# A hybrid block on one core: attention moved ahead by pairs of heads, the matrix memory moved beside W_out

## The chip, the cores and the metric

The kernel runs on one core of one Trainium2 chip. The time is that of one execution on the device, in microseconds; three runs gave 2598.55, 2602.10 and 2604.48 us, and their median, 2602.1 us, is the time before. The profile is one more execution, whose span is 2604.3 us. A difference of 0.2%, about 5 us, is the least that such runs tell from none.

## The reference, cut to what matters

All 2048 tokens are one sequence of width 1024, and everything is float32.

```
a = rmsnorm(x); u = a @ w_in
mq, mk, mv, mo, mi, mf, sq, sk, sv = split(u)    # 4 x 512, 2 x 4, 3 x 512 columns
mq, mk = silu(conv4(mq)), silu(conv4(mk))        # causal, 4 taps
hm = sigmoid(mo) * rmsnorm(mlstm(mq, mk, mv, mi, mf))   # 4 heads x 128, a matrix memory by chunks
hs = stick_breaking(sq, sk, sv)                  # 8 heads x 64, causal
h = x + concat(hm, hs) @ w_out
h = h + hier_moe(rmsnorm(h))                     # router, 32 experts, top 2 in one of 4 groups
h = h + sigmoid(rmsnorm(h) @ w_ple_gate) * rmsnorm(p @ w_ple_proj)
out = rmsnorm(h)
```

In the stick-breaking attention each score z gives a keep factor sigmoid(-z); a query's weight on a key is the difference of two running products of these factors, taken from the query backwards.

## The kernel before, in words

A float32 product that has to be exact is three products of TensorE in float32r: each operand is split into a rounded part and the rest (`split`, L79 a copy that rounds, on ScalarE; L80 a subtraction on VectorE), and `mm3` (L88 to L90) issues hi x hi, lo x hi, hi x lo. The normalised input, transposed and split, stays in SBUF as aTh and aTl for all projections.

`phase1`, in the order of TensorE's instructions: the transposes of x (L175) with the 32 units of `out_gate` between them (24 products of 260 columns each, the output gate and the memory's gates); `gates`, a chain of small transfers and running maxima; mq and mk, four heads each, 96 products of 512 columns a head, with a convolution on VectorE behind; mv, 32 units of 24 products of 256 columns. Then `stick_proj`: 12 weight chunks of 128 columns (q, k and v of four pairs of heads), 4 units of 24 products of 512 columns each, results to DRAM. A unit of these stands between the steps of `mlstm`, which goes through 16 chunks of 128 tokens in three steps each and writes its result to DRAM (hmh, hml). `load_w` holds two sets of split weights and loads one chunk ahead; those of `stick_proj` are issued by ScalarE (L116), others by SP.

`phase2` is the attention, 320 part-steps of 128 queries by up to 512 keys. A step of `front`: two products z (L579, L580), the sigmoid on ScalarE (L582), a mask on GpSimd for a diagonal block (L584), the running product by a scan on VectorE (L587). A step of `back` on the block before: four transposes (L600), the split (L79, L80), and two products with the differences of v (L612, L613). Blocks are 512 queries t by 512 keys s; heads come in the order (1, h), then (3, h) with the (0, h), then (2, h). Between heads stand tiles of W_out of 128 tokens whose 512 queries are done: 48 products of 512 columns (L88 to L90 into `pw`), 8 transposes (L557) and 8 products of the router (L561). The last tiles of W_out, the projection of p and the routing (`after_attention`) end at 1577 us; the experts (to 2399 us) and the last stage follow, and neither is touched.

[...]

Of the kernel before, what the change touches and what calls it, by code (L numbers as in the profile page):

```python
# [30 lines left out]
def f32(ap):  # L31
    return ap.bitcast(F32)


class Net:
    def __init__(self, ctx, tc, a, out):
# [9 lines left out]
        self.zeros = self.const.tile([P, TB], F32, name="zeros")  # L46
# [45 lines left out]
    # ---------------------------------------------------------------- projections  # L92
    def phase1(self):
        nc, tc, a = self.nc, self.tc, self.a
        self.q2 = self.mk("q2", [SH, P, S])          # rows: q_hi | q_lo of a head
        self.k2 = self.mk("k2", [SH, P, 2, S])       # [k_hi ; k_hi], [k_lo ; k_lo]
        self.dv2 = self.mk("dv2", [NT, P, SH, P])    # v[s-1] - v[s], hi | lo
        self.vend = self.const.tile([64, SH, NT], F32, name="vend")     # last v row of each token tile
# [4 lines left out]
        self.hmh = self.mk("hmh", [MH, P, S])  # L103
        self.hml = self.mk("hml", [MH, P, S])
        w_in = a["w_in"][0].rearrange("(c p) n -> p c n", p=P)
        with ExitStack() as st:
            ap_ = st.enter_context(tc.tile_pool(name="aT", reuse_waits="tile", bufs=1))
            pp = st.enter_context(tc.tile_pool(name="pp1", reuse_waits="tile", bufs=4, space=PSUM))
# [5 lines left out]
            def load_raw(wp, c0, n, width):  # L114
                raw = wp.tile([P, KC, width], F32, name="wraw", bufs=1)
                (nc.scalar if n == P else nc.sync).dma_start(raw[:, :, :n], w_in[:, :, c0:c0 + n])  # L116
                return raw
# [10 lines left out]
            def proj_dt(w, m, t):  # L128
                """[128 columns, 512 tokens]"""
# [6 lines left out]
                return ps  # L136

            def proj_td(w, n, i):
                """[128 tokens, n columns]"""
# [7 lines left out]
            G = self.G = self.const.tile([P, 2, NT, MH], F32, name="G")  # L147
            bg = self.const.tile([P, 8], F32, name="bg")
            nc.gpsimd.dma_start(bg, self.rows(a["b_gates"], 8))

            def load_x(xp, t):
                """512 tokens, normalised"""
# [8 lines left out]
            def norm_x(xp, xn):  # L161
                for xt in xn:
                    sq = xp.tile([P, D], F32, name="sq", bufs=1)
                    ss = self.small.tile([P, 1], F32, name="ss")
                    last = nc.scalar.activation(sq, xt, AF.Square, accum_out=ss)
                    r = self.rstd(ss, D, 1)
                    nc.vector.tensor_scalar(xt, xt, r, None, op0=ALU.mult)
                return last.ins

            def turn_x(ptp, xn, t):  # L170
                """a^T of 512 tokens"""
# [7 lines left out]
            # gates and output gate, values: [tokens, columns]  # L179
            with tc.tile_pool(name="w1", reuse_waits="tile", bufs=2) as wp:  # L180
                def out_gate(gp, w, h, i):
                    nv = 260 if h == 0 else 252
                    ps = proj_td(w, 260, i)
                    so = gp.tile([P, 260], F32, name="so", bufs=2)
# [7 lines left out]
                with tc.tile_pool(name="og", reuse_waits="tile", bufs=1) as gp, \  # L192
                        tc.tile_pool(name="xs", reuse_waits="tile", bufs=4) as xp, \
                        tc.tile_pool(name="pt1", reuse_waits="tile", bufs=4, space=PSUM) as ptp:
                    xn = load_x(xp, 0)
                    raw = load_raw(wp, O_MO, 260, 260)
                    last = norm_x(xp, xn)
                    gmh = gp.tile([P, MW], F32, name="gmh")
                    nc.gpsimd.dma_start(gmh, self.rows(a["g_mhead"], MW))
                    w2 = None  # L200
                    for t in range(NTB):
                        turn_x(ptp, xn, t)
                        if t == 0:
                            with tc.issue_after(last):
                                w = load_w(wp, O_MO, 260, 260, raw)
                        if t + 1 < NTB:
                            xn = load_x(xp, t + 1)
                            norm_x(xp, xn)
                        for i in range(4 * t, 4 * t + 4):
                            out_gate(gp, w, 0, i)  # L210
                            if t:
                                out_gate(gp, w2, 1, i - 4)
                        w2 = w2 or load_w(wp, O_MO + 260, 260, 260)
                    for i in range(NT - 4, NT):
                        out_gate(gp, w2, 1, i)
                mg = st.enter_context(tc.tile_pool(name="mg", reuse_waits="tile", bufs=1, side="right"))
                with tc.tile_pool(name="mgs", reuse_waits="tile", bufs=1, side="right") as ms, \
                        tc.tile_pool(name="cv", reuse_waits="tile", bufs=1, side="right") as cv:
                    w = load_w(wp, O_MQ, 256, 260)
                    gates = self.gates(mg, ms, pp)  # L220
                    next(gates)
                    for dst, off, cw, sc in ((self.mqs, O_MQ, "conv_q", 1.0), (self.mks, O_MK, "conv_k", float(P) ** -0.5)):
                        taps = cv.tile([P, 4, MH], F32, name="taps" + cw)
                        for j in range(4):
                            nc.sync.dma_start(taps[:, j], a[cw][0, j].rearrange("(h p) -> p h", p=P))
                        for h in range(2):
                            nxt = {(O_MQ, 0): O_MQ + 256, (O_MQ, 1): O_MK, (O_MK, 0): O_MK + 256, (O_MK, 1): O_MV}[off, h]
                            w2 = load_w(wp, nxt, 256, 260)
                            for m in range(2):
                                hd = 2 * h + m  # L230
                                raw = cv.tile([P, 3 + S], F32, name="cvraw")
                                nc.vector.memset(raw[:, 0:3], 0.0)
                                for t in range(NTB):
                                    ps = proj_dt(w, m, t)
                                    nc.scalar.copy(raw[:, 3 + t * TB:3 + (t + 1) * TB], ps)
                                acc = cv.tile([P, S], F32, name="cvacc")
                                nc.vector.tensor_scalar(acc, raw[:, 0:S], taps[:, 0, hd:hd + 1], None, op0=ALU.mult)
                                for j in range(1, 4):
                                    nc.vector.scalar_tensor_tensor(acc, raw[:, j:j + S], taps[:, j, hd:hd + 1], acc,
                                                                   op0=ALU.mult, op1=ALU.add)  # L240
                                next(gates, None)
                                sg = raw[:, 3:]
                                nc.scalar.activation(sg, acc, AF.Sigmoid)
                                nc.vector.scalar_tensor_tensor(acc, acc, sc, sg, op0=ALU.mult, op1=ALU.mult)
                                nc.sync.dma_start(dst[hd * P:(hd + 1) * P, :], acc)
                            w = w2
                sw = st.enter_context(tc.tile_pool(name="sw", reuse_waits="tile", bufs=2, side="right"))
                with tc.tile_pool(name="mvp", reuse_waits="tile", bufs=2) as vpool:
                    for h in range(2):
                        if h == 0:  # L250
                            w2 = load_w(wp, O_MV + 256, 256, 260)
                        else:
                            w, w2 = w2, load_w(sw, O_SQ, P, P)
# [1061 lines left out]
```

## Time and profile before

| | |
|---|---|
| median of the runs | 2602.1 us (2598.55 to 2604.48) |
| profiled execution, span | 2604.3 us, 36320 instructions |
| TensorE busy | 2440.4 us, 94% |
| VectorE busy | 1718.2 us, 66% |
| ScalarE busy | 1296.2 us, 50% |
| GpSimd busy | 658.9 us, 25% |
| read and written | 385.44 MB and 114.39 MB |

The profile counts an engine as busy while at least one of its instructions runs. A product on TensorE is recorded until its result is out, and the next starts before that, so that the spacing of products, not their recorded length, says what one costs. "Idle before" is the time an engine did nothing before an instruction, with what ended it. The span falls into stages by TensorE's work: 0 to 412 us the input, the output gate, mq, mk and mv; 412 to 770 `stick_proj` and the matrix memory; 770 to 1515 the attention with W_out; and the untouched rest.

### The profile page before, as it was taken

What the parts mean: (1) busy time and instruction counts of PE and PEld (TensorE: products, weight loads), DVE (VectorE), ACT (ScalarE), POOL (GpSimd) and SP (SyncE); (2) the same over time, 40 slices, a digit from 0 to 9 for tenths busy, and PEclk for the clock granted to TensorE, in tenths of its full rate; (3) what the DMA queues carried; (4) which work ended last, traced back from release to release, by engine and by line L of the source; (5) the groups of instructions that cost most, each with busy time, mean ns of one, the idle gap of its engine ahead of it and who ended that gap; (6) DMA issues with size and microseconds to landing.
All of it is one profiled execution on the core that took longest, in us unless ns stands there. A gap on an engine that the chain in (4) does not pass through costs nothing. (4 is left out here: it accounts for less than half of the span.)

```text
span 2604.3 us, 36320 instructions
## 1 busy us (share of the span) xinstructions
PE 2440.4 (94%) x12620; PEld 1986.2 (76%) x12620; DVE 1718.2 (66%) x2623; ACT 1296.2 (50%) x2249; POOL 658.9 (25%) x777
## 2 busy tenths in 40 slices
PE   7989999999987898889999998999999999998998
PEld 7968899888776666666777776778877778776887
DVE  4335412444549999998787566877677778776665
ACT  5322212322336666656454355666566667665443
POOL 2200000100113333322222122332332233231664
PEclk9999999999998999999999998999999999999999
DMA  5231125677766566555555548999999899998332
GB/s 181 90 47 71 66 88 144 186 207 219 211 158 158 152 157 163 139 138 144 146 146 142 146 154 274 305 309 312 299 281 327 285 307 313 310 309 268 131 132 97
DMA packets 333013, 502.25 MB, mean 193 GB/s; under 512 B 39644, under 2 KB 176988, under 8 KB 331804
## 3 DMA queue, kind: packets, MB, share of 16 engines
q1 hardware_dynamic: 210540, 338.57, 39.5%
q0 software_dynamic: 97616, 123.05, 20.6%
q10 hardware_dynamic: 24672, 38.29, 4.2%
q8 instruction: 100, 1.64, 0.3%
q14 instruction: 85, 0.70, 0.1%
HBM read 385.44 MB, written 114.39 MB: 192 GB/s over the span
## 5 line engine op out<-in xcount | busy, mean ns | idle before, releaser
L80 DVE TENSOR_TENSOR wl<-wraw,wh 128x1024 fp32r<-128x1024 f32 x384 | 457.9, 1218 | 122.1 <-ACT wh L79 118.6
L79 ACT CAST wh<-wraw 128x1024 fp32r<-128x1024 f32 x384 | 396.8, 1051 | 214.9 <-DMA wraw<-in_w_exp_up_dram 66.4
L88 PE MATMUL ppx<-wh,xh 128*128 128x512 f32 x816 | 330.2, 405 | 2.1 <-ACT wh L79 1.6
L90 PE MATMUL ppx<-wh,xl 128*128 128x512 f32 x816 | 323.4, 397 | 2.8 <-DVE xl L80 2.7
L89 PE MATMUL ppx<-wl,xh 128*128 128x512 f32 x816 | 322.5, 396 | 0.5 <-DVE wl L80 0.5
L88 PE MATMUL ps<-aTh,whi 128*128 128x512 f32 x640 | 255.2, 399 | 0.0
L89 PE MATMUL ps<-aTl,whi 128*128 128x512 f32 x640 | 254.8, 398 | 0.0
L90 PE MATMUL ps<-aTh,wlo 128*128 128x512 f32 x640 | 254.1, 397 | 0.0
L600 PE MATMUL pt<-ident,prod 128*128 128x128 f32 x1088 | 191.8, 289 | 61.5 <-DVE pl L80 55.5
L587 DVE TENSOR_TENSOR_SCAN prod<-keep,prod,zeros 128x512 f32<-128x512 f32 x192 | 244.2, 1273 | 1.7 <-ACT keep L582 0.6
L600 PEld LDWEIGHTS pt<-ident,prod 128*128 128x128 f32 x1088 | 124.8, 143 | 149.8 <-DVE pl L80 132.6
L79 ACT CAST ph<-pt 128x512 fp32r<-128x512 f32 (+1 forms) x320 | 166.7, 522 | 141.0 <-PE pt L600 137.7
L582 ACT ACTIVATE keep<-pz 128x512 f32<-128x512 f32 (+2 forms) x320 | 170.7, 536 | 58.9 <-PE pz L580 38.3
L80 DVE TENSOR_TENSOR pl<-pt,ph 128x512 fp32r<-128x512 f32 (+1 forms) x320 | 186.3, 585 | 5.7 <-ACT ph L79 5.5
L90 PEld LDWEIGHTS ppx<-wh,xl 128*128 128x128 f32 x816 | 154.5, 189 | 40.5 <-DVE xl L80 5.4
L88 PEld LDWEIGHTS ppx<-wh,xh 128*128 128x128 f32 x816 | 154.6, 189 | 36.5 <-ACT wh L79 2.0
L89 PEld LDWEIGHTS ppx<-wl,xh 128*128 128x128 f32 x816 | 154.8, 190 | 33.4 <-DVE wl L80 1.0
L1105 POOL DMA_INDIRECT h<-y,tokd x47 | 125.7, 2675 | 161.1 <-DVE y L1104 61.0
L88 PE MATMUL ps<-whi,aTh 128*128 128x260 f32 (+1 forms) x512 | 145.7, 285 | 0.0
L89 PE MATMUL ps<-wlo,aTh 128*128 128x260 f32 (+1 forms) x512 | 144.8, 283 | 0.0
L90 PE MATMUL ps<-whi,aTl 128*128 128x260 f32 (+1 forms) x512 | 143.7, 283 | 0.0
L72 POOL TENSOR_TENSOR rs_r<-rs_v,neghalf 128x1 f32<-128x1 f32 (+1 forms) x80 | 56.4, 705 | 338.6 <-DVE rs_v L70 315.4
(320 smaller groups left out, 5413.1 us busy)
## 6 DMA issues: line engine op xcount, KB each, us to landing
wraw<-in_w_exp_gate_dram SPq DMA_DIRECT2D x128, 512.0 KB
wraw<-in_w_exp_up_dram SPq DMA_DIRECT2D x128, 512.0 KB
wraw<-in_w_exp_down_dram SPq DMA_DIRECT2D x128, 512.0 KB
kt<-k POOLq DMA_DIRECT2D x80, 512.0 KB, 4.8
dv<-dv POOLq DMA_DIRECT2D x80, 256.0 KB, 3.5
k<-pst SPq DMA_DIRECT2D x64, 256.0 KB
q<-pst SPq DMA_DIRECT2D x32, 256.0 KB
dv<-pst SPq DMA_DIRECT2D x16, 512.0 KB
```

Of the source, the lines that this page charges most:

```text
L72: nc.gpsimd.tensor_tensor(r, v, self.neghalf[:, :width], op=ALU.pow)
L79: first = nc.scalar.copy(hi, src)
L80: nc.vector.tensor_sub(lo, src, f32(hi))
L88: mm(ps, lh, rh, start=start, stop=False)
L89: mm(ps, lh, rl, start=False, stop=False)
L90: return mm(ps, ll, rh, start=False, stop=stop)
L582: self.sig = nc.scalar.activation(kk[:, :w], ps[:, :w], AF.Sigmoid, scale=-0.125)
L587: nc.vector.tensor_tensor_scan(pr[:, :w][:, ::-1], kk[:, :w][:, ::-1], self.zeros[:, :w], 1.0 if s == t else carry[j][:, 0:1], ALU.mult, A ...
L600: nc.tensor.transpose(pt[:, i * P:(i + 1) * P], pr[i][:, j * P:(j + 1) * P], self.ident)
L1105: nc.gpsimd.indirect_dma_start(out=self.hd_[:, :], out_offset=bass.IndirectOffsetOnAxis(ap=idx[:n], axis=0), in_=y[:n], in_offset=None, co ...
```

## The change

Five parts.

1. Attention stands first and goes by pairs of heads. After the input, only pair 0 is projected. Then `attention` takes pair m, all four t and both heads, and behind each z product a planner (`fill`) issues the next pair's projections in pieces of three products: 1.45 pieces a step, 1.8 in the last pair, where the pieces are those of mq. A new product tile every 8 pieces, 96 pieces a pair, 128 for mq. The attention's result goes to DRAM (sbh, sbl), one store pair for each pair of heads and t.
2. Weights inside the attention have one buffer: one raw half (128 x 4 x 128), one whi, one wlo. All weight loads are on SP, in halves.
3. Output gates, the convolutions of mq, `gates`, mk and mv come after the attention.
4. The matrix memory's chunks stand between the quarters of W_out's tiles; its result stays in SBUF. Tile i uses chunk i; a router's part comes one tile later than its tile. Attention's results are loaded again by GpSimd (`load_mix`), and W_out's weights are loaded at the start of this stage.
5. The scan's addend is one column of zeros read with stride 0 instead of a tile of 512 columns.

`after_attention` is the same text, but takes a piece of the projection of p at every yield of the last tiles, and a tile now yields five times instead of twice: 20 transposes and 19 products of p stand before the last router's products.

```diff
-
-            def load_w(wp, c0, n, width, raw=None):
-                raw = raw or load_raw(wp, c0, n, width)
-                hi = wp.tile([P, KC, width], F32R, name="whi")
-                lo = wp.tile([P, KC, width], F32R, name="wlo")
+            def load_w(wp, c0, n, width, wbufs=2, rbufs=2):
+                hi = wp.tile([P, KC, width], F32R, name="whi", bufs=wbufs)
+                lo = wp.tile([P, KC, width], F32R, name="wlo", bufs=wbufs)
                 for h in range(2):
                     s = slice(4 * h, 4 * h + 4)
-                    self.split(hi[:, s, :n], lo[:, s, :n], raw[:, s, :n])
+                    raw = wp.tile([P, 4, width], F32, name="wraw", bufs=rbufs)
+                    nc.sync.dma_start(raw[:, :, :n], w_in[:, s, c0:c0 + n])
+                def pair_proj(m):
+                    for kind, o in enumerate((O_SQ, O_SK, O_SV)):
+                        w = load_w(wp, o + P * m, P, P, 1, 1)
+                        yield None
+                        old = [None]
+                        for t in range(NTB):
+                            yield from unit(pp, stg, ptv, w, kind, m, t, old)
+
...
+                self.attention(sp, kp, pz, pt_, po, [pair_proj(1), pair_proj(2), pair_proj(3), mq_proj()])
...
+                w = load_w(wp, O_MO + 260, 260, 260)
+                w2 = load_w(wp, O_MO, 260, 260)
+                for i in range(NT):
+                    out_gate(w, 1, i)
+                    if i % 8 == 4:
+                        conv_q(i // 8)
...
+    def attention(self, sp, kp, pz, pt_, po, filler):
...
+        zeros = self.zeros[:, 0:1].to_broadcast([P, TB])
...
+        def fill(m):
+            steps["done"] += 1
+            due = steps["done"] * RATE[m]
+            while steps["given"] < due:
+                steps["given"] += 1
+                next(filler[m], None)
+
+        def step(part, m):
+            for j in range(4):
+                if part:
+                    part(j)
+                if m is not None:
+                    fill(m)
...
+        RATE = (1.45, 1.45, 1.45, 1.8)
...
+                mix = [kp.tile([P, TB], F32R, name=f"mix{u}", bufs=1) for u in range(2)]
+                for e in range(2):
+                    h = 2 * m + e
+                    qt = kp.tile([P, TB], F32R, name="qt", bufs=2)
+                    nc.gpsimd.dma_start(qt, self.q2[m][e, :, t * TB:(t + 1) * TB])
+                    carry = None
+                    for s in range(t, -1, -1):
+                        carry, dv, part = front(t, h, s, qt, carry)
+                        step(part, m)
+                        f = back(t, h, s, carry, dv, mix)
+                        turns.extend((*f, j) for j in range(4))
+            for _ in filler[m]:
                 pass
...
-            nc.sync.dma_start(self.hmh[:, :, tk].rearrange("h p t -> p h t"), f32(hh_))
-            nc.sync.dma_start(self.hml[:, :, tk].rearrange("h p t -> p h t"), f32(hl_))
+            out.append((hh_, hl_))
...
+                        if e == 3:
+                            yield
                     nc.vector.tensor_tensor(xt[:, ns], xt[:, ns], ps, op=ALU.add)
+                    if n == 0:
+                        yield
...
+            hms = []
+            ml = self.mlstm(mw, mps, self.mg, hms)
+            for k in range(KC):
+                load_wo((k + MH) % KC)
+            for _ in range(4):
+                next(ml)
+            load_consts()
+            tiles = {}
+            for i in range(NT - 1):
+
+                tiles[i] = f = wout_tile(i, hms[i])
+                next(f)
+                next(ml)
+                next(f)
+                if i:
+                    next(tiles[i - 1])
+                next(ml)
+                next(f)
+                if i:
+                    next(tiles[i - 1])
+                next(f)
+                next(ml)
+            for _ in ml:
+                pass
+            mem.close()
+            self.mctx.close()
+            self.after_attention(cp, pw, [tiles[NT - 2], wout_tile(NT - 1, hms[NT - 1])])
```

TensorE in the attention, first before, then after. pt, ot and pz are the transposes', the outputs' and the scores' tiles; ps is a projection's.

```order
L613 MATMUL ot<-pl,dv 128x512
L579 MATMUL pz<-kt,qt 128x512
L580 MATMUL pz<-kt,qt 128x512
L612 MATMUL ot<-ph,dv 128x512
L600 MATMUL pt<-ident,prod_10776 128x128
L600 MATMUL pt<-ident,prod_10791 128x128
L600 MATMUL pt<-ident,prod_10809 128x128
L600 MATMUL pt<-ident,prod_10827 128x128
```

```order
L398 MATMUL pt<-ident,prod_1278 128x128
L398 MATMUL pt<-ident,prod_1296 128x128
L398 MATMUL pt<-ident,prod_1320 128x128
L398 MATMUL pt<-ident,prod_1351 128x128
L410 MATMUL ot<-ph,dv 128x512
L411 MATMUL ot<-pl,dv 128x512
L377 MATMUL pz<-kt,qt 128x512
L378 MATMUL pz<-kt,qt 128x512
L88 MATMUL ps<-aTh,whi 128x512
L89 MATMUL ps<-aTl,whi 128x512
L90 MATMUL ps<-aTh,wlo 128x512
```

Before, one step's products stand alone. After, a step has two pieces of a projection, six products, behind its scores.

The weights' loads in the order of the queue that issues them, before (ScalarE; vt is a copied result of mv, whi the rounded weights).

```order
L116 DMA wraw<-in_w_in_dram 128x8x128
L257 COPY vt<-ps 128x256
L79 CAST whi<-wraw 128x512 x2
L116 DMA wraw<-in_w_in_dram 128x8x128
L257 COPY vt<-ps 128x256 x2
L79 CAST whi<-wraw 128x512 x2
```

A whole chunk of 1024 rows is loaded in one transfer, ahead of the unit that uses it. After, on SP, with k, q and dv the projected results and sbh and sbl the attention's:

```order
L122 DMA wraw<-in_w_in_dram 128x4x128
L189 DMA k_2_80<-pst 128x1x512 x4
L425 DMA sbh<-mix_3271 128x512
L425 DMA sbl<-mix_3272 128x512
L189 DMA k_2_80<-pst 128x1x512 x8
L122 DMA wraw<-in_w_in_dram 128x4x128
L189 DMA k_2_80<-pst 128x1x512 x4
L122 DMA wraw<-in_w_in_dram 128x4x128
L209 DMA dv_2_84<-pst 128x4x256
```

A half of a chunk's weights stands ahead of the last results of the chunk before and the other half behind them.

SP at the end of the attention, after: the last results, the taps of the convolutions, the first weights of the output gate.

```order
L425 DMA sbh<-mix_8629 128x512
L425 DMA sbl<-mix_8630 128x512
L308 DMA tapsconv_q<-in_conv_q_dram 128x4x1 x4
L308 DMA tapsconv_k<-in_conv_k_dram 128x4x1 x4
L122 DMA wraw<-in_w_in_dram 128x4x260 x2
```

The output gate's weights stand behind the store of the last result and eight small loads.

## Rows read from the trace of the kernel before

**Rows 1.** Windows by stage: stretch, length, engines' busy us (instructions), PE clock, DMA share, GB/s.

```profile
0.00:412.00 412.00, 385.62 (x2441) 347.45 (x2442) 153.42 (x183) 121.31 (x199) 36.47 (x57) 0.98 0.29 88
412.00:770.00 358.00, 347.88 (x1843) 293.38 (x1842) 162.32 (x457) 108.25 (x323) 30.37 (x38) 0.99 0.71 194
770.00:1515.00 745.00, 668.11 (x3525) 511.36 (x3524) 622.18 (x993) 413.91 (x798) 216.63 (x370) 0.98 0.59 149
```

**Rows 2.** Windows of one kind of product: 512 columns, then 256 columns.

```profile
195.30:260.40 65.10, 65.10 (x282) 52.66 (x282) 34.89 (x21) 14.20 (x17) 0.00 (x0) 1.00 0.19 71
...
325.50:390.60 65.10, 65.10 (x556) 65.10 (x555) 11.98 (x10) 12.65 (x28) 0.00 (x0) 1.00 0.28 88
```

**Rows 3.** Timeline of one full attention step: start, us, engine, line, operation, [idle before].

```profile
999.96 1.27 DVE L587 TENSOR_TENSOR_SCAN prod<-keep,prod,zeros 128x512 f32<-128x512 f32 x1
...
1000.10 0.66 PE L600 MATMUL pt<-ident,prod 128*128 128x128 f32 x4 [0.30 <-DVE pl L80]
...
1000.51 0.48 PE L613 MATMUL ot<-pl,dv 128*128 128x512 f32 x1
...
1000.83 0.40 PE L580 MATMUL pz<-kt,qt 128*128 128x512 f32 x1
...
1001.06 0.39 PE L612 MATMUL ot<-ph,dv 128*128 128x512 f32 x1
...
1001.15 0.67 DVE L80 TENSOR_TENSOR pl<-pt,ph 128x512 fp32r<-128x512 f32 x1
...
1001.29 0.39 PE L579 MATMUL pz<-kt,qt 128*128 128x512 f32 x1
1001.74 1.28 DVE L587 TENSOR_TENSOR_SCAN prod<-keep,prod,zeros 128x512 f32<-128x512 f32 x1
...
1001.87 0.66 PE L600 MATMUL pt<-ident,prod 128*128 128x128 f32 x4 [0.19 <-DVE pl L80]
```

**Rows 4.** PE timeline of a W_out tile's end, between attention steps.

```profile
1258.66 1.98 PE L561 MATMUL pwt<-wr,cT 128*128 128x36 f32 x16
1260.46 0.52 PE L600 MATMUL pt<-ident,prod 128*128 128x128 f32 x3
```

**Rows 5.** Timeline of one chunk of the matrix memory, PE and DVE rows.

```profile
565.41 0.38 PE L437 MATMUL mp<-C,mq 128*128 128x129 f32 x2
...
567.72 0.61 PE L437 MATMUL mp<-C,mq 128*128 128x129 f32 x4
...
573.48 1.14 DVE L466 SCALAR_TENSOR_TENSOR mhm<-mhm,rs_r,mo 128x128 f32<-128x128 f32 x4 [1.13 <-POOL rs_r L72]
```

**Rows 6.** Groups by shape, 412 to 770 us: busy, mean ns, idle before.

```profile
L80 DVE TENSOR_TENSOR wlo<-wraw,whi 128x512 fp32r<-128x512 f32 x20 | 13.6, 694 | 29.1 <-ACT whi L79 29.0
L79 ACT CAST whi<-wraw 128x512 fp32r<-128x512 f32 x20 | 12.1, 621 | 32.8 <-PE ps L89 29.1 <-DMA hml<-mhl 3.7
```

**Rows 7.** Windows of 5 us around the wait for the gates.

```profile
150.00:155.00 5.00, 3.27 (x15) 2.27 (x13) 0.18 (x1) 0.00 (x0) 0.00 (x0) 1.00 0.10 4
155.00:160.00 5.00, 0.00 (x0) 0.00 (x0) 0.00 (x0) 0.00 (x0) 0.00 (x0) 0.65 0.00 0
160.00:165.00 5.00, 2.45 (x7) 1.93 (x8) 2.25 (x4) 1.59 (x4) 0.00 (x0) 0.50 0.06 13
```

**Rows 8.** DMA issues of the attention: KB each, median us to landing.

```profile
kt<-k POOLq DMA_DIRECT2D x80, 512.0 KB, 4.8
dv<-dv POOLq DMA_DIRECT2D x80, 256.0 KB, 3.5
```

**Rows 9.** The convolution's taps, four small loads on SP: ns of one issue.

```profile
L225 SPq DMA_DIRECT2D tapsconv_q<-in_conv_q_dram x4: 383/503/509, 132.8 to 134.3; - x4
```

**Rows 10.** DVE groups by shape, 780 to 1235 us.

```profile
L621 DVE SCALAR_TENSOR_TENSOR osum<-ot,vend,otmp 64x128 f32<-64x128 f32 x96 | 26.7, 335 | 0.4
...
L80 DVE TENSOR_TENSOR mix<-osum,mix 64x512 fp32r<-64x512 f32 x24 | 16.4, 681 | 0.4
...
L80 DVE TENSOR_TENSOR wol<-wst,woh 128x1024 fp32r<-128x1024 f32 x8 | 9.9, 1237 | 3.4 <-ACT woh L79 3.3
```

More of the change, by code (lines that the diff above doesn't have):

```diff
@@ L190, in out_gate @@
                             nc.vector.tensor_add(G[:, g, i, :], ps[:, 252 + 4 * g:256 + 4 * g], bg[:, 4 * g:4 * g + 4])
[L192 to L253, printed above, removed]
-                        for i in range(NT):
-                            ps = proj_td(w, 256, i)
-                            vt = vpool.tile([P, 256], F32, name="vt")
-                            nc.scalar.copy(vt, ps[:, :256])
-                            nc.sync.dma_start(self.mvs[i * P:(i + 1) * P, 256 * h:256 * h + 256], vt)
@@ L308, in phase1, with values @@
-            units = stick_proj(w2)
-            ml = self.mlstm(st, mg)
-            next(units)
-            for i in range(3 * NT):
-                if i % 8 != 7:
-                    next(units, None)
-                next(ml)
-            next(units)
-            next(ml)
-            for _ in units:
-                pass
+                def values(w, h, i):
+                    ps = proj_td(pp, w, 256, i)
+                    vt = gp.tile([P, 260], F32, name="so")
+                    nc.scalar.copy(vt[:, :256], ps[:, :256])
+                    nc.sync.dma_start(self.mvs[i * P:(i + 1) * P, 256 * h:256 * h + 256], vt[:, :256])
@@ new lines, in phase1, with conv @@
+                taps = []
+                for cw in ("conv_q", "conv_k"):
+                    tp = cv.tile([P, 4, MH], F32, name="taps" + cw)
+                    for j in range(4):
+                        nc.sync.dma_start(tp[:, j], a[cw][0, j].rearrange("(h p) -> p h", p=P))
+                    taps.append(tp)
+                def conv(raw, tp, hd, dst, sc):
+                    acc = cv.tile([P, S], F32, name="cvacc")
+                    nc.vector.tensor_scalar(acc, raw[:, 0:S], tp[:, 0, hd:hd + 1], None, op0=ALU.mult)
+                    for j in range(1, 4):
+                        nc.vector.scalar_tensor_tensor(acc, raw[:, j:j + S], tp[:, j, hd:hd + 1], acc,
+                                                       op0=ALU.mult, op1=ALU.add)
+                    sg = raw[:, 3:]
+                    nc.scalar.activation(sg, acc, AF.Sigmoid)
+                    nc.vector.scalar_tensor_tensor(acc, acc, sc, sg, op0=ALU.mult, op1=ALU.mult)
+                    nc.sync.dma_start(dst[hd * P:(hd + 1) * P, :], acc)
@@ new lines, in phase1 @@
+                w = load_w(wp, O_MK, 256, 260)
+                for i in range(NT):
+                    out_gate(w2, 0, i)
+                    if i % 8 == 4:
+                        conv_q(2 + i // 8)
+                gates = self.gates(mg, ms, pp)
+                next(gates)
+                for h in range(2):
+                    w2 = load_w(wp, O_MV if h else O_MK + 256, 256, 260)
+                    for m in range(2):
+                        hd = 2 * h + m
+                        raw = cv.tile([P, 3 + S], F32, name="cvraw")
+                        nc.vector.memset(raw[:, 0:3], 0.0)
+                        for t in range(NTB):
+                            for ps in proj_dt(pp, w, m, t):
+                                pass
+                            nc.scalar.copy(raw[:, 3 + t * TB:3 + (t + 1) * TB], ps)
+                        conv(raw, taps[1], hd, self.mks, float(P) ** -0.5)
+                    next(gates, None)
+                    w = w2
@@ L422, in mlstm @@
             if done:
-                finish(*done)
+                finish(done)
             nc.vector.tensor_tensor(dd, dd, ps, op=ALU.mult)
@@ L626, in phase2 @@
-            turns = []
-            late = []
-            wq = []
-            begun = False
-            def step(part):
-                for j in range(4):
-                    if part:
-                        part(j)
-                    if len(turns) > (LAG if part else 0):
-                        turn, mult, i = turns.pop(0)
-                        turn(i)
-                        late.append((mult, i))
-                        while len(late) > 2:
-                            f, i = late.pop(0)
-                            f(i)
@@ L644, in phase2 @@
-            mixes, count = {}, 0
-            def head(t, h):
-                if t not in mixes:
-                    mixes[t] = [(mp if t in (1, 2) else mp2).tile([P, MH, TB], F32R, name=f"mix{u}") for u in range(2)]
-                qt = kp.tile([P, TB], F32R, name="qt", bufs=2)
-                nc.gpsimd.dma_start(qt, self.q2[h, :, t * TB:(t + 1) * TB])
-                carry = None
-                for s in range(t, -1, -1):
-                    carry, dv, part = front(t, h, s, qt, carry)
-                    step(part)
-                    f = back(t, h, s, carry, dv, mixes[t])
-                    turns.extend((*f, j) for j in range(4))
@@ L675, in phase2 @@
-            for _ in range(2):
-                step(None)
-            for f, i in late:
-                f(i)
-            att.close()
-            self.after_attention(cp, pw, wq)
+            hms = []
[19 more added lines that the diff above has]
+                next(ml)
```

407 lines of the change are left out of this document (230 added, 177 removed).

## The prediction

> **What bounds the kernel now.** I read the stage windows first [rows 1]. TensorE is busy 94% in all, and up to 770 us nothing else comes near it; from 770 to 1515 it is busy 668 of 745 us, and there VectorE has 622. But a busy TensorE is not a full one, so I cost its work by spacing. Where nothing interrupts, 282 products of 512 columns fill 65.10 us, 0.231 each, and 556 of 256 columns fill 65.10, 0.117 each [rows 2]. A full attention step [rows 3] has four transposes (1000.10 to 1000.51, 0.41), one product that costs 0.32 because it follows transposes, and three at 0.23: 1.42 us. It takes 1.77, since the next transposes wait for VectorE: scan, subtraction and next scan start at 999.96, 1001.15 and 1001.74, so 1.19 + 0.59 = 1.78. So in the attention the reader is to see VectorE set the pace and TensorE wait 0.36 a step.
>
> The sum of TensorE's work up to the last product of W_out, by these spacings:
> - to 412 us: output gate 768 x 0.119 = 91, mq and mk 768 x 0.231 = 177, mv 768 x 0.117 = 90, transposes of x 128 x 0.10 = 13: 371, lost 41. [...]
> - to 770 us: 1152 x 0.231 = 266, v's 64 transposes 5, and the matrix memory, which is what is left of the busy 348: 77, or 4.9 a chunk: 349, lost 9.
> - to 1515 us: attention 192 x 1.42 = 273 and 128 diagonal steps at 0.94 (by their columns) = 121; 16 tiles of W_out at 48 x 0.231 + 8 x 0.10 + 1.8 for the router [rows 4], with its changes of operand 14.2, = 227; in all 624 with 3 for drains, lost 121.
>
> So 171 us are lost before 1515, and 121 of them where VectorE sets the pace.
>
> **The change, part by part, as a new timeline up to the last product of W_out.**
>
> Phase 0: the transposes 13, pair 0's projections 288 x 0.231 = 66, its v transposes 2: 81. It loses the 41 of today less the gates' hole, 29: 110. Pair 1's first weights need the only buffer, which the last unit of pair 0 still reads: load, cast, subtraction, 10 by the durations below.
>
> Attention: its own work 394, three pairs' projections 199 with 5 of transposes, mq 384 x 0.231 = 88: 686. A step now has 1.45 x 0.69 = 1.0 of projection behind its scores, so TensorE needs 2.42 where VectorE needs 1.78, and the 0.36 vanishes. What is late next:
> - The pieces run out: 96 + 3 loads at 1.45 a step last 71 of 80 steps in pairs 0 to 2, and mq's 128 at 1.8 some 73. The some 34 steps left over are paced as now: 34 x 0.36 = 12.
> - Weights. Nine changes of chunk happen in the attention. The second half of a chunk can only be fetched when the first is split, as there is one raw half, and both splits wait until the old chunk's last products have read whi and wlo. A 128x512 cast takes 0.62 and the subtraction 0.69 [rows 6]; this trace has no fetch of 256 KB of weights alone, and the nearest, 256 KB of dv, takes 3.5 to land [rows 8]. First half: 0.62 + 0.69 less the attention step issued between, about 1.2 lost. Second half: 0.69 + 3.5 + 0.62 + 0.69 = 5.5 less the first half's 12 products and a step, 4.0: 1.5. Bounds: nothing, if the steps between hide all, to 6.1 with no cover. I take 2.7 each, near the middle as part of the cover is in the trace: 24.
> - The last drain 3, and 3% of the work for jitter between two nearly full engines: 21. No row shows that; the bounds are 0 and the 121 lost today, and I take a little over twice the 9 of the stage in which projections and matrix memory share TensorE.
>
> VectorE's load bears on that. Per pair: 48 x 1.78 + 32 diagonal steps at 0.63 of it = 122; the outputs, 8 x (4 x 0.28 + 0.68) = 14 with waits 16 [rows 10]; the projections' and weights' splits 15. That is 153 against TensorE's 171, so it is 89% and hidden. The scan's addend with stride 0 is not in the trace: from half (it then is as a plain two-operand instruction, 0.67 beside 1.27 [rows 3]) to 10% more, which would add 8 to 153 and still be hidden; I take no change, worth nothing here either way. Attention: 686 + 60 = 746.
>
> End of the attention: the output gate's weights stand on SP behind the last result's store and eight loads of taps at 0.503 each [rows 9]. Store 3.7, taps 4, load 4, cast and subtraction 1.3, less drained work, and then some time at the lower clock: 15 (from 5, if SP's queue runs ahead, to 25).
>
> Gates, mk, mv: 91 + 88 + 90 = 269, and 2: 271. The chain of the gates now lies beside mk, 88 of products, so its hole is gone.
>
> W_out with the matrix memory: 227 + 78 + 3 = 308. The chain of a chunk, from the last product on the old state to the finished rows, is 567.72 to 574.62, 6.9 us [rows 5]; what is issued between is half a tile or more, 11 to 12.7 us, so it hides. The start does not: W_out's weights, eight pieces with 1.24 of subtraction each [rows 10], come when aT is free, with the first chunk's chain: 18. And 15 x 0.6 for the changes of bank and the router: 9. Together 335. Loads of attention's results on GpSimd come a tile ahead, at no cost; were they late, at 3.5 to 4.8 each [rows 8], two tiles' start would show it.
>
> Sum: 110 + 10 + 746 + 15 + 271 + 335 = 1487. Then the last router's products, which the routing waits for, come behind 20 transposes and 19 products of p, 20 x 0.10 + 19 x 0.231 with a change of operand: 7. It is work that has to be done anyway, but the routing's chain behind the router is as long as before, so I let it count in full. 1494 against 1515: -21 on the span of 2604.3 gives 2583; the profiled execution is 2.2 over the median, so 2581 for the median. Its own range: the unknowns (switches 0 to 55, end 5 to 25, jitter 0 to 45, start of W_out 9 to 27) do not go wrong together: 2560 to 2600.
>
> [...] The subtraction of a weight chunk waits 29 us for its cast and that waits for TensorE, not for a transfer [rows 6]: weights have been early. [...]
>
> **Rivals.**
> 1. Everything is covered: neither switches nor jitter (24 + 21) cost anything, which the window to 770 us speaks for, where projections between chain steps lose 9 in 358 [rows 1]. Against it: there the weights had two buffers. 2536.
> 2. The other side: VectorE's queue. Projection splits stand between the scans in program order, and each waits for ScalarE's cast of its unit. The 48 units' splits then hold back the scan behind them, the transposes behind it and TensorE by a cast, 0.62: 30 us, 2611. For it: 89% load. Against it: two blocks' products are buffered, so a late scan need not be seen at once. It decides when the attention loses more than 81 in place of 60, 12% of its work.
> 3. Weights in full: nine switches at 6.1, 55 in place of 24: 2612. For it: SP's order, in which the second half stands behind 4 to 8 stores of results that wait for their own splits. Against it: TensorE has attention steps in its order in the meantime, though it can't jump over a projection that waits.
> 4. The clock: an idle stretch of 5 us is followed by one at 0.50 today [rows 7]. If each of nine switches and the two ends brings 2 us of loss, 22: 2603, no change. Against it: the attention before has an idle moment in every step, and its stage has 0.98 all the same [rows 1].
> 5. Matrix memory paced: if the three stages of a chunk take 24 us beside a tile in place of 19.7 because ScalarE and GpSimd answer both, 15 x 4.3 = 65: 2646. For it only that the loop is in strict order; against it the 6.9 us chain.
>
> **How the numbers follow.** Forecast 0.45 (2581), rival 1 0.18 (2536), rival 2 0.14 (2611), rival 3 0.10 (2612), rival 4 0.08 (2603), rival 5 0.05 (2646). A measurement here tells 0.2%, about 5 us, from none. Faster: nearly all of the forecast (0.42), rival 1 and 0.03 of rivals 2 to 4, which may be half true: 0.63. Same: most of rival 4, the top of the forecast's range and the milder side of rivals 2 and 3: 0.11. Slower: the rest, 0.26. The range leaves out the lower half of rival 1, rival 5 and the far end of 2 and 3: 2536 to 2622.
>
>
> **What would show it.** The attention (first scores to last result) at 746 us, 686 if rival 1, 776 or more if 2 or 3; VectorE in it at 82% of the time. Idle of TensorE before the first product of a chunk with the cast or the subtraction of weights as releaser, 24 us in all: 0 speaks for rival 1, 55 for rival 3; before transposes, with VectorE as releaser, under 35 us, over 60 for rival 2. The granted clock above 0.97 outside the ends, below for rival 4. A period of 20 us for a tile and a chunk. The last product of W_out at 1487. If that stands at 1487 and the span still differs, the error is in the tail.

## The result and the profile after

The changed kernel takes 2559.1 us (median of four runs, 2556.3 to 2559.7) where the kernel before took 2602.9 beside it: ratio 0.9836, interval 0.9822 to 0.985. That is 43.8 us faster, twice the 21 that were forecast. The stated range of 2536 to 2622, which takes in most of the rivals, holds it; the forecast's own range of 2560 to 2600 ends just above it. The profiled execution has a span of 2557.8 us, 46.5 under the one before.

By stage, with the boundaries moved to where the stages now lie (columns as in [rows 1]):

```profile
0.00:115.70 115.70, 94.69 (x449) 76.45 (x450) 51.81 (x103) 53.24 (x90) 13.34 (x28) 0.97 0.62 175
115.70:824.90 709.20, 686.03 (x3648) 556.48 (x3646) 611.18 (x905) 413.81 (x790) 182.68 (x317) 1.00 0.63 161
824.90:845.00 20.10, 6.32 (x29) 6.01 (x29) 7.71 (x10) 3.31 (x4) 0.00 (x0) 0.58 0.67 182
845.00:1109.00 264.00, 258.92 (x1794) 240.54 (x1793) 103.38 (x99) 61.94 (x102) 39.88 (x32) 0.99 0.28 90
1109.00:1130.00 21.00, 12.88 (x110) 12.71 (x109) 2.21 (x3) 4.44 (x8) 4.60 (x13) 0.87 0.57 139
1130.00:1469.00 339.00, 304.62 (x1764) 259.90 (x1764) 173.49 (x515) 103.00 (x318) 57.22 (x75) 0.96 0.62 172
```

The second row is the attention with the projections between its steps: TensorE is busy 686 of 709 us at a granted clock of 1.00, and VectorE 611. The third is the hole before the output gate, in which TensorE has nothing to do. The last one is W_out with the matrix memory, in which TensorE is idle 34 us. Against the forecast's timeline:

| stretch | forecast | measured |
|---|---|---|
| to the first scores | 120 | 115.7 |
| attention | 746 | 709 |
| hole to the output gate's first product | 15 | 14.0 |
| gates, mk, mv (to about 1121.8) | 271 | 283 |
| W_out with the matrix memory, its start included | 335 | 345 |
| last product of W_out at | 1487 | 1466.6 |
| from there to the experts' first transposes, against before | +7 | +4.3 (66.5 against 62.2) |

What TensorE waited for, in the attention (waits in us, how many, the longest):

```profile
PE pt L398 <- DVE pl L80: 10.1, 33, 0.7
PE ptv L206 <- DVE dvT L202: 8.8, 12, 1.1
...
PE ot L410 <- issue: 1.0, 4, 0.3
PE ps L88 <- ACT whi L79: 0.8, 1, 0.8
PE ps L90 <- DVE wlo L80: 0.7, 4, 0.2
```

and in W_out's stage:

```profile
PE pwt L710 <- ACT cT L711: 15.8, 12, 1.8
PE pw L88 <- DMA sb<-sbh: 8.1, 1, 8.1
PE mps L547 <- DVE mhm L619: 7.8, 1, 7.8
PE mps L591 <- POOL md L578: 7.3, 1, 7.3
PE mp L590 <- DMA mq<-mqs: 1.3, 1, 1.3
```

The wait of a step's transposes for the split is 10.1 us. Before, it was 55.5 in the stage of [rows 3], by the group of these transposes there. The second line is the transposes of a W_out tile, whose wait for the copy cT was 1.8 us before:

```profile
L600 PE MATMUL pt<-ident,prod 128*128 128x128 f32 x1088 | 191.8, 289 | 61.5 <-DVE pl L80 55.5 <-DVE prod L587 3.3
...
L557 PE MATMUL pwt<-ident,wst 128*128 128x128 f32 x120 | 20.0, 277 | 1.8 <-ACT cT L558 1.8
```

Waits for weights (whi, wlo) are 1.5 us where 24 were forecast. These are idle times; by the spacing of the products a short wait costs about 0.2 us more than its idle time, since a product of 512 columns is recorded for 0.39 us and the next starts after 0.23 (one behind an idle time of 0.17 starts at 157.48, 0.57 after the one before it). In W_out's stage three waits are its start, 7 to 8 us each, for the attention's result (sb), the first chunk's masked scores (md) and the first finished rows (mhm). A fourth, for the copy of a tile's transposes (cT), comes with nearly every tile.

### The profile page after: what moved, and what is told of

Same layout as the page of the kernel before. It is cut to its first block, busy times and chain, and to the rows that moved or that the text cites. A ratio compares the mean times of both kernels' runs of the same rounds, so it can differ in the third digit from the quotient of the medians.

```text
span 2557.8 us, 36511 instructions
## 1 busy us (share of the span) xinstructions
PE 2403.7 (94%) x12620; PEld 1987.6 (78%) x12620; DVE 1731.0 (68%) x2628; ACT 1294.0 (51%) x2243; POOL 657.5 (26%) x777
## 4 chain that ended last, share of the span: by engine, by line
PE 43%; DMA 11%; ACT 3%; issue 3%; DVE 3%; POOL 1%; SPq 0%; ACTq 0%; DVEq 0%; POOLq 0%
PE ppx L90 7%; PE ppx L88 7%; PE ppx L89 7%; DMA wraw<-in_w_exp_gate_dram 3%; DMA wraw<-in_w_exp_down_dram 3%; PE ps L88 2%; PE ps L90 2%; PE ps L89 2%; DMA md<-gr 2%; PE pw L89 2%; PE pw L90 2%; PE pw L88 2%; DMA wraw<-in_w_exp_up_dram 2%; ACT wh L79 2%; DVE wl L80 1%
## 5 line engine op out<-in xcount | busy, mean ns | idle before, releaser
L88 PE MATMUL ppx<-wh,xh 128*128 128x512 f32 x816 | 329.7, 405 | 5.8 <-ACT wh L79 5.0
L90 PE MATMUL ppx<-wh,xl 128*128 128x512 f32 x816 | 323.2, 396 | 2.8 <-DVE xl L80 2.7
L88 PE MATMUL ps<-aTh,whi 128*128 128x512 f32 x640 | 257.5, 403 | 6.6 <-ACT whi L79 3.3
L90 PE MATMUL ps<-aTh,wlo 128*128 128x512 f32 x640 | 255.0, 398 | 0.7 <-DVE wlo L80 0.7
L385 DVE TENSOR_TENSOR_SCAN prod<-keep,prod,zeros 128x512 f32<-128x512 f32 x192 | 245.0, 1276 | 11.3 <-PE pt L398 5.8
L80 DVE TENSOR_TENSOR pl<-pt,ph 128x512 fp32r<-128x512 f32 (+1 forms) x320 | 190.1, 594 | 46.5 <-ACT ph L79 46.1
L90 PEld LDWEIGHTS ppx<-wh,xl 128*128 128x128 f32 x816 | 154.1, 189 | 41.0 <-DVE xl L80 6.3
L88 PEld LDWEIGHTS ppx<-wh,xh 128*128 128x128 f32 x816 | 154.4, 189 | 40.0 <-ACT wh L79 5.3
L398 PE MATMUL pt<-ident,prod 128*128 128x128 f32 x1088 | 173.0, 274 | 11.6 <-DVE pl L80 10.1
L398 PEld LDWEIGHTS pt<-ident,prod 128*128 128x128 f32 x1088 | 134.0, 139 | 61.6 <-DVE pl L80 23.6
L370 POOL DMA_DIRECT2D dv<-dv x80 | 60.9, 761 | 413.1 <-PE ot L411 338.6
L1174 POOL DMA_INDIRECT h<-y,tokd x47 | 119.8, 2550 | 164.1 <-DVE y L1173 63.4
L88 PE MATMUL ps<-whi,aTh 128*128 128x260 f32 (+1 forms) x512 | 145.0, 285 | 13.8 <-ACT whi L79 13.8
L88 PEld LDWEIGHTS ps<-aTh,whi 128*128 128x128 f32 x640 | 121.5, 190 | 32.6 <-ACT whi L79 4.3
L90 PEld LDWEIGHTS ps<-aTh,wlo 128*128 128x128 f32 x640 | 121.6, 190 | 31.2 <-DVE wlo L80 3.5
```

The source lines that it names most:

```text
L80: nc.vector.tensor_sub(lo, src, f32(hi))
L88: mm(ps, lh, rh, start=start, stop=False)
L90: return mm(ps, ll, rh, start=False, stop=stop)
L370: nc.gpsimd.dma_start(dv, self.dv2[m][4 * s:4 * s + 4, :, e, :].rearrange("i p d -> p i d"))
L385: nc.vector.tensor_tensor_scan(pr[:, :w][:, ::-1], kk[:, :w][:, ::-1], zeros[:, :w], 1.0 if s == t else carry[j][:, 0:1], ALU.mult, ALU.add)
L398: nc.tensor.transpose(pt[:, i * P:(i + 1) * P], pr[i][:, j * P:(j + 1) * P], self.ident)
```

## The experiments

All are edits of the changed kernel, and their stage lengths come from their own profiles. The kernel as it is, run again beside the last two, took 2560.7 us (2557.2 to 2565.6; ratio 0.9846, 0.9827 to 0.9865). From the experts' first transposes to TensorE's last product, which no edit touches, these profiles take from 1014 to 1025 us, so a change of a few us is read from its stage.

**Projections ahead of the steps.**

```
-        RATE = (1.45, 1.45, 1.45, 1.8)
+        RATE = (200, 200, 200, 200)
```

> The same work, but the next pair's projections are all issued at the first step of a pair, not behind its steps. Theory A (the projections between the steps fill what TensorE waited for VectorE): the attention alone is paced by VectorE, 138 us a pair, 552 in all, the projections' 292 come on top, and the eight changes of weights that now have only 12 products as cover lose 2.7 each: some 865 in place of 709, less what runs over at the borders of the pairs, so 2690 to 2720 us. Theory B (the attention gained because W_out's tiles and the old order of heads have left it): its 686 us of TensorE's work stay packed, no more than 2575.

2676.7 us, ratio 1.028 (1.0262 to 1.0298): slower than before the change. The attention takes 826 us in place of 709, with the waits for VectorE back:

```profile
PE pt L398 <- DVE pl L80: 58.5, 153, 1.2
PE pt L398 <- DVE prod L385: 19.2, 24, 1.0
```

Theory A holds in kind, but the stage grew by 117 us where 157 were the sum and 131 to 161 the stated range. The weights' 22 us did not come at all (waits for whi 1.2 us), and attention steps still run while a pair's projections are under way. At a change of chunk they stand between the last product on the old weights (L90) and the first on the new (L88), though the code issues them behind:

```profile
160.69 0.40 PE L90 MATMUL ps<-aTh,wlo 128*128 128x512 f32 x1
160.93 0.38 PE L398 MATMUL pt<-ident,prod 128*128 128x128 f32 x2
...
164.68 0.48 PE L377 MATMUL pz<-kt,qt 128*128 128x512 f32 x1
165.07 0.50 PE L88 MATMUL ps<-aTh,whi 128*128 128x512 f32 x1
```

So attention work stands in the gap, 4 us of it here.

**Pieces over all 80 steps.**

```
-        RATE = (1.45, 1.45, 1.45, 1.8)
+        RATE = (1.25, 1.25, 1.25, 1.67)
```

> The pieces are spread over all 80 steps of a pair: 1.25 a step (1.67 in the last pair) in place of 1.45 (1.8). Theory A (TensorE's 10 us of waits for the split of the attention are the 34 steps that are left when the pieces have run out): most of them go, 2549 to 2553 us. Theory B (they are jitter of two nearly full engines, anywhere in a pair): 2557 to 2561, with the same 10 us.

2563.6 us, ratio 0.9838 (0.9817 to 0.986); the attention 706.6 us against 708.9. The wait for the split fell, and others came:

```profile
PE ptv L206 <- DVE dvT L202: 4.9, 9, 0.8
PE pt L398 <- DVE pl L80: 4.2, 8, 0.8
PE ot L410 <- ACT ph L79: 3.9, 3, 1.3
PE ot L410 <- issue: 2.9, 9, 0.4
PE ps L90 <- DVE wlo L80: 2.9, 4, 0.8
```

So 6 of the 10 us were the steps left over, as theory A has it, but the stage is only 2 us shorter. In the time nothing is seen; theory A's 2549 to 2553 us did not come.

**Every half of the weights fetched twice** (attention only; wbufs is 1 there).

```
+                    for _ in range(2 if wbufs == 1 else 1):
-                    nc.sync.dma_start(raw[:, :, :n], w_in[:, s, c0:c0 + n])
+                        nc.sync.dma_start(raw[:, :, :n], w_in[:, s, c0:c0 + n])
```

> Each half of a chunk's weights inside the attention is fetched twice in a row into its one buffer, so that a fetch takes about 8.4 us in place of 4.2. A change of chunk then has its second half split 0.69 + 8.4 + 0.62 + 0.69 = 10.4 us after the first. Theory A (the cover is the four pieces on the first half, spread over 4 / 1.45 = 2.8 steps of 2.42 us or of 1.9 on diagonals, 5.4 to 6.7 us, which is why 5.5 us had cost nothing): 3.7 to 5 us are late at each of some nine changes, 33 to 45 in all, 2592 to 2604 us, with TensorE waiting for wlo and whi. Theory B (weights are not on TensorE's way at all, since attention steps can be put ahead of a late projection): under 2566 us. By the prediction's own cover of 4.0 us it would be 6.4 a change, 58, about 2617.

2621.7 us, ratio 1.0062 (1.0039 to 1.0086). The attention takes 764.5 us, 55.6 more. TensorE waits ten times for whi, 3.2 us in the mean:

```profile
PE ps L88 <- ACT whi L79: 32.4, 10, 4.4
```

That is a little under theory A's 3.7 to 5 a change; theory B falls. The time is above theory A's 2592 to 2604 us and near the one by the prediction's own cover (58 us more), but for another reason, the clock. The attention as a whole, and windows of 5 us around the longest wait (columns as in [rows 1]):

```profile
118.50:883.00 764.50, 709.61 (x3658) 573.08 (x3656) 613.62 (x906) 414.49 (x791) 179.76 (x317) 0.97 0.62 159
...
413.00:418.00 5.00, 4.96 (x30) 3.93 (x29) 4.72 (x7) 2.85 (x6) 1.97 (x4) 1.00 1.07 265
418.00:423.00 5.00, 0.62 (x2) 0.53 (x3) 1.38 (x3) 1.11 (x2) 1.03 (x3) 0.73 1.02 264
423.00:428.00 5.00, 5.00 (x16) 3.84 (x15) 1.87 (x3) 0.59 (x1) 0.20 (x1) 0.59 0.39 88
428.00:433.00 5.00, 4.84 (x27) 3.85 (x26) 4.16 (x8) 2.86 (x5) 0.00 (x0) 1.00 0.07 19
```

After a wait of 4.4 us TensorE works on at a granted clock of 0.59, and from 424.46 to 427.02 its products stand 0.43 us apart in place of 0.23. Of the 55.6 us, 32 are waits. The other 23 are TensorE's busy time, 709.6 us in place of 686.0 for the same work, at a mean granted clock of 0.97 in place of 1.00. Up to 573 us there are six stretches in which TensorE is idle for 3 us or more, and in the next window of 5 us the granted clock is 0.50 to 0.79. The fall of the mean by 0.03 is 21 us on 709.6, so by this estimate these 23 us are in the main work at a lower clock.

**Two banks for the transposes before the router.**

```
-                    pt = pw.tile([P, 4, P], F32, name="pwt", bufs=1)
+                    pt = pw.tile([P, 4, P], F32, name="pwt", bufs=2)
...
-            ps = pp.tile([P, 2, 2, P], F32, name="plt", bufs=2)
+            ps = pp.tile([P, 2, 2, P], F32, name="plt", bufs=1)
```

> The transposes before the router get two PSUM banks in place of one (and the transposes of p in the tail one in place of two, for room). Theory A (in the stage of W_out with the matrix memory the second four transposes wait for the copy of the first four out of the one bank, 15.8 us in 12 tiles): 2544 to 2548 us, a period of 18.8 us for a tile and a chunk in place of 20.1. Theory B (the chain of the chunk sets the period, and takes what the transposes give): 2556 to 2560, other waits in their place.

2541.1 us, ratio 0.976 (0.9745 to 0.9775). That is theory A, and a little more: W_out's stage from its first product is 319.8 us against 336.6, and no wait for cT is left:

```profile
PE mps L547 <- DVE mhm L619: 8.4, 1, 8.4
PE pw L88 <- DMA sb<-sbh: 8.0, 1, 8.0
PE mps L591 <- POOL md L578: 7.0, 1, 7.0
PE mps L601 <- DVE mhl L80: 1.9, 3, 0.9
```

**The taps behind the weights, and at the very start.** In one kernel the eight loads stand behind `load_w` of the output gate in the code. In the other two loads in phase 0 take their place, as this cut shows:

```
+                    if t == 2:
+                        taps = []
...
+                            nc.sync.dma_start(tp, a[cw][0].rearrange("j (h p) -> p j h", p=P))
```

> The eight loads of the convolutions' taps are issued behind the output gate's weights in place of ahead of them. Theory A (after the attention the weights wait in SP's queue, where the eight loads take 4.3 us): the hole before the first product of the output gate falls from 13.8 to some 9.3 us, 2554 to 2555 us. Theory B (the weights wait for the SBUF that the attention's last steps give back): 13 to 14 us of hole and 2558 to 2560 us.

> The convolutions' taps are loaded at the very start, in two transfers in place of eight, so that after the attention only the store of the last result stands ahead of the output gate's weights. If the eight issues are what the weights wait for, the hole before the first product falls from 13.8 us (11.3 with four of them left) to 9 to 9.6, and the time to 2548 to 2551 us. If the weights wait for room in SBUF, the hole stays above 11.

2551.4 us (0.9794, 0.9778 to 0.981) and 2556.8 us (0.9827, 0.981 to 0.9845). The hole was 11.3 and 12.7 us of waiting, against 13.8 in the changed kernel: less came than the theories of the eight loads say. The other theories, of room in SBUF, fall too, as the weights are issued earlier in both. SP's queue at this place in the changed kernel, with the taps behind, and with the taps at the start:

```profile
833.30 0.92 SPq L122 DMA_DIRECT2D wraw<-in_w_in_dram  x2
```

```profile
829.91 2.11 SPq L327 DMA_DIRECT2D tapsconv_q<-in_conv_q_dram  x4
832.07 1.05 SPq L122 DMA_DIRECT2D wraw<-in_w_in_dram  x2
833.16 3.54 SPq L327 DMA_DIRECT2D tapsconv_k<-in_conv_k_dram  x4
```

```profile
827.62 0.32 SPq L424 DMA_DIRECT2D sbh<-mix  x1
828.34 0.32 SPq L424 DMA_DIRECT2D sbl<-mix  x1
828.75 0.40 SPq L324 DMA_DIRECT2D cvraw<-mqr  x1
829.21 12.41 SPq L122 DMA_DIRECT2D wraw<-in_w_in_dram  x4
```

Behind the weights in the code, four of the eight loads still come ahead of them in the queue. Counted from the attention's last product, the weights are issued 2.4 us earlier than in the changed kernel and cast 2.4 us earlier, so for these four loads theory A is right. With the taps at the very start SP issues another load ahead of the weights, 1024 KB of mq. The weights start 4 us earlier than in the changed kernel and are cast only 1 us earlier (836.73 against 837.75), so it looks like the bytes ahead that they wait for; that load was not moved by itself.

From the attention's end to W_out's first product both take some 8 us less, 297.6 and 297.3 us against 305.3. A part is the waits of gates and mk for ScalarE, below, which fall from 5.1 to 1.6 and 0.2 us. In the changed kernel a convolution's sigmoid of 1.9 us stands on ScalarE just ahead of them (at 933.40); that the convolutions' place makes the difference is likely, but was not tried.

**The matrix memory's first chunk ahead of W_out's loads.**

```
-            for k in range(KC):
-                load_wo((k + MH) % KC)
             for _ in range(4):
                 next(ml)
+            for k in range(KC):
+                load_wo((k + MH) % KC)
```

> At the start of W_out's stage the first chunk of the matrix memory (and the first step of the second) is issued ahead of the loads and splits of W_out, not behind. Theory A (its start loses time because VectorE's and ScalarE's orders put eight splits of W_out, which wait for 4 MB to land, ahead of the first chunk's steps: 7.3 us for md and 7.8 for the first finished rows): the chain runs while W_out lands, and 8 to 13 us of these waits go, 2546 to 2551 us. Theory B (what the stage starts on is the landing of W_out itself, so that only the releaser changes): 2556 to 2560 us.

2560.3 us (2552.4 to 2563.2), ratio 0.9843 (0.9829 to 0.9856): nothing in the time, 5.0 us in the stage (331.6 against 336.6). The wait for md went from 7.3 to 1.6 us, that for the first finished rows from 7.8 to 11.0. This is mostly theory B: one of the two waits went, and the other grew by half of it.

**Together.**

> Two banks for the transposes before the router and the taps loaded at the start, in one. If the two act in different stages, their gains add: in the trace 17.5 us less in W_out's stage and 8 less from the end of the attention to W_out, so 23 to 27 us less than the changed kernel, 2532 to 2536 us.

> The same with the matrix memory's first chunk issued ahead of W_out's loads. If the 5 us that this gave in W_out's stage are its own, 2527 to 2532 us; if they were the wait that the two banks take away, or the run's scatter, as e9, 2532 to 2536 us.

> The changed kernel as it is, on the chip of the next two: 2556 to 2560 us, as before. Any theory.

The kernel with banks and taps took 2541.6 us (0.9769, 0.9748 to 0.9789), that with all three edits 2534.6 (0.975, 0.9731 to 0.9768; 2531.4 to 2539.3). In the profiles the gains add: the last product of W_out comes at 1440.7 and 1436.8, 26 and 30 us earlier than in the changed kernel, and W_out's stage goes from 319.7 to 315.1 us with the third edit, nearly the 5 us that it gave alone. In the time of the first of the two they do not: it is not below the two banks alone (0.976) and misses its 2532 to 2536 us, as its profile loses 9 us again in the experts (1024.5 us). The time with all three lies in the range that stood for no gain of the third edit; but the two intervals overlap, and only the stage shows that edit. The version with all three beats both kernels: 66 us under the kernel before, 26 under the changed one.

## Why the prediction was right, and what was mis-sized

The mechanism was right, and the time lies in the range with the help of errors that offset each other. In the profile the attention came out 37 us shorter than forecast, the two stages behind the hole 22 us longer up to the last product of W_out, and the rest 10 us shorter in small parts: 25 us under the forecast's span.

**The start.** The sum of phase 0 takes 12 us for the hole at the gates, a term that no run shows as such. The kernel before waits 9.3 us there (to 162.55), and its products behind that stand 0.43 us apart in place of 0.23 up to 166.40 (the clock of [rows 7]), so about 11 by an estimate from these. The first scores came at 115.7 us where 120 were forecast.

**The pace of the attention.** Right. VectorE set it, 1.0 us of projection a step covers it, and without that cover the waits return (826 us). VectorE's load was put at 153 us a pair and is 611.2 / 4 = 152.8. TensorE's work was put at 686 by spacing, and its busy time, which is not quite the same thing, is 686.0. VectorE's 86% of the stage hides, so rival 2 falls.

**Weights: the step that failed.** "Second half: 0.69 + 3.5 + 0.62 + 0.69 = 5.5 less the first half's 12 products and a step, 4.0". This and "about 1.2 lost" for the first half made 24 us of nine changes. The 5.5 was nearly right (5.7 below, from 156.75 to 162.46), the cover was not. It counted the first half's products as if they came in one run with one attention step. At 1.45 pieces a step, the four pieces on the first half are spread over 2.8 steps. One change of chunk in the changed kernel (start, us, engine, line):

```profile
155.55 0.62 ACT L79 CAST whi<-wraw 128x512 fp32r<-128x512 f32 x1
156.68 0.39 PE L88 MATMUL ps<-aTh,whi 128*128 128x512 f32 x1
156.75 0.67 DVE L80 TENSOR_TENSOR wlo<-wraw,whi 128x512 fp32r<-128x512 f32 x1
...
157.45 0.39 SPq L122 DMA_DIRECT2D wraw<-in_w_in_dram  x1
...
158.21 0.45 PE L88 MATMUL ps<-aTh,whi 128*128 128x512 f32 x1
...
158.95 0.39 PE L88 MATMUL ps<-aTh,whi 128*128 128x512 f32 x1
...
160.86 0.40 PE L88 MATMUL ps<-aTh,whi 128*128 128x512 f32 x1
161.12 0.62 ACT L79 CAST whi<-wraw 128x512 fp32r<-128x512 f32 x1 [0.95 <-DMA wraw<-in_w_in_dram]
161.77 0.69 DVE L80 TENSOR_TENSOR wlo<-wraw,whi 128x512 fp32r<-128x512 f32 x1 [0.16 <-ACT whi L79]
162.58 0.39 PE L88 MATMUL ps<-aTh,whi 128*128 128x512 f32 x1
```

The pieces start at 156.68, 158.21, 158.95 and 160.86, with attention between, the fifth at 162.58; the second half is split by 162.46. The cover is 5.9 us and just enough: 1.5 us of waits in all where 24 were put down, and 32 once the fetch is doubled. So rival 3 falls: with fetches of this length (157.45 to 161.12 here) the one buffer of part 2 costs no more than these 1.5 us. The first half, for which 1.2 was put down, waits 0.17 here; the prediction's own terms, 0.62 + 0.69 less a step of 1.42, leave nothing.

That the spreading by RATE alone gives the cover is not shown. With the pieces in one lump (the first experiment) the waits for whi are 1.2 us too, since attention steps stand in the gap. What covers a change is attention work between the pieces, and either way it was there.

**Jitter and leftovers.** 21 and 12 were allowed; all waits of the attention together, the weights' included, are 23 us by its idle time, 10.1 of them for the split. 8.8 us are v's transposes waiting for VectorE (L206), which the sum did not have.

**Rival 1** (everything covered, 2536) was thus nearly right inside the attention: 746 without its 24 and 21 is 701, and 709 were measured. New waits behind it made up most of the difference:

- **Gates, mk and mv**, 12 us more than forecast. TensorE waits 1.9 and 3.2 us, at the gates and at mk's first product, for ScalarE, and works at a lower clock behind the hole and behind these waits (0.53 in 840 to 845 us, 0.63 in 940 to 945). The hole itself has the forecast's length: the store, the taps (issued from 828.66 to 832.97) and the weights' landing (4.3 us) are in it.
- **W_out with the matrix memory**, 10 more. The start costs 25 us of waits (sb 8.1, mq 1.3, md 7.3, the first finished rows 7.8) where 18 was put down, and the "0.6" a tile is 15.8 of waits for cT alone. This rested on the kernel before [rows 4], where attention steps stood between a tile's eight transposes and hid the copy out of the one bank; there the wait was 1.8 us in 15 tiles. With them gone only a few products of W_out stand there, the wait is open, and a second bank took 16.8 us out of the stage. The 6.9 us chain of a chunk [rows 5] is hidden as forecast, so rival 5 falls: a tile with its chunk takes 20 us, where 24 would have been its pace.
- **The tail**: 8.7 us from W_out's last product to the router's are added, where 7 were put down as work. Of them 3.8 are waits of the transposes of p for its loads (before, there are none). At the experts' first transposes 4.3 are left; at their first product it is 6.9 again, behind a wait of 5.0 us for split weights in place of 1.6. Which of the two counts for the time was not tried.

**Rival 4**: the attention's granted clock is 1.00, so rival 4 falls there; at the ends behind the attention it holds, as the clocks of 0.53 and 0.63 show. With the doubled fetch it holds at the changes of weights too: with waits of 3.2 us in the mean the attention's granted clock is 0.97.

In these traces the order on an engine is not simply that of the code. The load of mq that took the taps' place (828.75, the weights at 829.21), the four taps that stayed ahead of the weights (829.91 and 832.07), and the attention steps among the lumped projections (160.93 to 165.07) all stand ahead of instructions that the code issues first.

## What to carry to other kernels

When an engine waits in every step for another, put independent work of its own between the steps in small pieces. The same mixture can hide a single-buffered load: compare the refill (fetch and split, 5.7 us here) with the time from the first to the last use of the half before it (5.9 us here), with all that stands between the uses. Work that is moved away had been hiding something: list the short waits that stood beside it (here the copy cT out of one bank, 1.8 us before and 15.8 after) and give each its second buffer in the same change. Cost a wait of a few us with what comes after it: behind one of 4.4 us the granted clock was 0.59 here.

## What the runs showed of the hardware

With the weights fetched twice, ten waits of 3.2 us in the mean, the attention took 55.6 us more, not 32.4, and behind the six idle stretches of 3 us or more up to 573 us the granted clock of the next 5 us is 0.50 to 0.79. Behind the wait of 3.2 us that ended at 125.52 the fall comes when TensorE is already at work again: its products stand 0.29 us apart at 126.58, 0.43 from 126.87 to 129.86, and 0.23 again from 131.25. The waits of the changed kernel's attention, 1.1 us at most, leave the granted clock at 1.00. The scan with its addend read at stride 0 takes 1.276 us a 128x512 block, against 1.273 before.
